# Sample loads and raw tokens issued earlier, key transposes later, and other PSUM banks for the first accumulators of the last part, in a two-layer decoder step

## The chip, the cores and the metric

The kernel runs on one core of one Trainium2 chip. The metric is the device time of one launch in microseconds, and the numbers of the kernel before are the median and the extremes of three runs, beside one execution that the hardware profiler recorded.

## What is computed

One inference step of a decoder with two layers, for 1024 prompt tokens and 8 samples that share all weights. Layer 0 has a gated linear recurrence (HGRN2, four heads of 128), layer 1 a stick-breaking attention over keys and values that layer 0 left; both have, beside it, a cross-attention of four heads into 256 memory rows, and a SwiGLU after it. The reference in short:

```python
def mem_attend(q, mk, mv):
    s = jnp.einsum('blhd,bmhd->bhlm', q, mk) * (q.shape[-1] ** -0.5)
    p = jax.nn.softmax(s, axis=-1)
    return jnp.einsum('bhlm,bmhd->blhd', p, mv)

def swiglu(h, w_gu, w_down):
    gate, up = jnp.split(h @ w_gu, 2, axis=-1)
    return (jax.nn.silu(gate) * up) @ w_down
...
    mk_p, mv_p = jnp.split(jnp.einsum('bmd,lde->lbme', mem_prompt, w_mem_kv), 2, axis=-1)
...
    for l in range(DEPTH):
        hn = rmsnorm(h, g[0])
        if l < N_A:
            mix, S = a_mixer(hn, w_in_a[l], ...)
        else:
            mix = b_mixer(hn, w_in_b[l - N_A], ...)
        h = h + rmsnorm(mix, g[1])
        h = h + rmsnorm(swiglu(rmsnorm(h, g[2]), w_gu[l], w_down[l]), g[3])
```

The prompt attends to memory keys and values projected from `mem_prompt`; each of the 8 samples has its own cached memory keys and values, and its own two pages of shared keys and values. All is float32.

## The kernel before

The tokens are two groups: group 0 is the first 512 prompt tokens, group 1 the last 512 and the 8 samples, 520 columns. Activations lie transposed, features on the partitions, in 8 tiles of 128 features. Every weight matrix is read in blocks of 512 rows by 128 columns (`w`), and each block is split into a high and a low half: `split_w` (L196) issues the DMA on SP, ACT casts (L206) and VectorE subtracts (L207). Activations are split likewise (L226 to L228). A product is then three matmuls, high by high, high by low and low by high, and a projection of 512 columns (`proj`, matmuls at L220) takes 24 matmuls for each of its output tiles and each half of the input features.

The order of the work is written out. Each stage is a generator that yields after each piece, and `weave` (L1617 to L1673) runs several generators side by side, each with a number of steps by which their pieces are spread over each other. The tile framework then makes one queue for each engine from it, and each engine works through its queue in order, waiting at semaphores. Three properties of the queues matter here:

- SP issues nearly all loads and stores, in order. A load whose tile is still in use holds all loads behind it.
- A tile comes from a pool of few buffers, taken in turn: T has 3 tiles, B 7, N 2, C 4, A 8; weights 5 raw and 5 split.
- PSUM has 8 banks: two pairs for projections (`mm`), three small ones (`s`, handed out by S()) and one for norms (`ns`). In the last part these pools are closed, and a pool called quads takes the same banks: q0 to q3, two of each.

The stages that the change touches:

- **Memory keys**, `mem_keys` (L815), once for each layer in the first core stage. A head's keys are 24 matmuls (L823) into one half of an `mm` pair. ACT copies them to a T tile (L828), and SP stores the tile (L829). PE then transposes the two halves of the copy into the other half of the same pair (L831), VectorE copies the result to another T tile (L833), and SP stores that to the output (L834).
- **First residual**, `residual` with `first` (L381). In layer 0 the residual stream is the raw input, which lies by tokens. Four loads of 128 tokens, 512 KB each (L388), are followed by a loop over the 8 feature tiles: four transposes into the norm bank (L396), an update by VectorE (L397) and an addition of the bank (L399). For group 1 the loads are at the start of the loop, after the key and value projections of group 0 and their stores.
- **Samples**, `sample_scores` (L935) and `sample_pv` (L960). A sample's scores are a product of its 256 cached keys with its query, broadcast to all partitions. For each of the 8 samples the loop loads the keys into a C tile (L1000 from the pages, L1014 from the memory cache), broadcasts the query by DMA into a B tile, multiplies (L954) and sums (L955) on VectorE; `sample_pv` does likewise with the values (L966, L967) and ends in matmuls (L969). These loops are woven with the feed-forward part of group 0 and, in layer 1, with the stick-breaking attention of the prompt. Of that, L1422 makes scores on PE, VectorE sums them along (L1440) and multiplies (L1443), PE transposes the result (L1449) and multiplies by the values (L1461).
- **Start of the last part.** `token_rows` and the final norms use L272, which sums squares with a matrix of ones, L283, which accumulates these squares on VectorE, and L416, which takes a projection out of its bank into the residual rows. `gate_up_q` (L468) makes the gate and the up half of a feed-forward block: `Q(0)`, `Q(1)` hold the gate's accumulators, `Q(2)`, `Q(3)` the up half's, and the matmuls are at L479.

The prediction also names the rows `w_in_a` and `w_gu`, the weights of the first projections and of the feed-forward part.

Of the kernel before, what the change touches and what calls it, by code (L numbers as in the profile page):

```python
# [9 lines left out]
F32 = mybir.dt.float32  # L10
# [8 lines left out]
P = 128  # L19
# [5 lines left out]
def tile_decoder(  # L25
# [6 lines left out]
    nc = tc.nc  # L32
# [348 lines left out]
    def residual(g, R, rstd, gc, store, acc=None, first=False):  # L381
        n = NG[g]
        w = D // 2 if first else n
        ht = [xpool.tile([P, 2, w], F32, tag=f"x{g}", name=nm("ht")) for _ in range(ND // 2)]
        for j in range(ND // 2):
            if first:
                t0 = g * G + j * P
                nc.sync.dma_start(ht[j].rearrange("p a n -> p (a n)"), x_prompt[0, t0 : t0 + P, :])  # L388
            else:
                nc.sync.dma_start(ht[j], hs[g][:, 2 * j : 2 * j + 2, :n])  # L390
        for k in range(ND):
            if first:
                ps = NS()
                for tb in range(CH):
                    xf = ht[tb].rearrange("p a n -> p (a n)")
                    nc.tensor.transpose(ps[:, tb * P : (tb + 1) * P], xf[:, k * P : (k + 1) * P], ident)  # L396
            nc.vector.scalar_tensor_tensor(R[k][:, :n], R[k][:, :n], gc(k), rstd[:, :n], op0=ALU.mult, op1=ALU.mult)  # L397
            if first:
                nc.vector.tensor_add(R[k][:, :G], R[k][:, :G], ps)  # L399
                if g:  # L400
                    nc.vector.tensor_add(R[k][:, G:n], R[k][:, G:n], xsraw[:, k, :])
            else:
                nc.vector.tensor_add(R[k][:, :n], R[k][:, :n], ht[k // 2][:, k % 2, :])
            if store:
                nc.sync.dma_start(hs[g][:, k, :n], R[k][:, :n])
            if acc is not None:
                sq_acc(acc, R[k][:, :n], k, n)
            yield
# [11 lines left out]
    class out_proj:  # L420


        def __init__(self, g, l, store, last=False):
            self.g, self.l, self.store, self.x, self.last = g, l, store, [], last
# [11 lines left out]
        def finish(self):  # L436
# [3 lines left out]
            yield from residual(g, self.R, rstd, lambda k: gcol(l, 1, k), not self.last, acc, l == 0)  # L440
# [27 lines left out]
    def gate_up_q(l, f, xt):  # L468

        h, n = PW[1], NG[1]  # L470
        sg = T()
        for j in range(2):
            w = split_w(w_gu[l], 0, ND, j * DFF + f * P)
            pp = [Q(2 * j + a) for a in range(2)]
# [340 lines left out]
    def mem_keys(l):  # L815
        for h in range(H):
            w = split_w(w_mem_kv[l], 0, ND, h * P)
            pb = mmp.tile([P, 2, 512], F32, tag="mm", name=nm("mm"))
            ps, pt = pb[:, 0, :], pb[:, 1, :]
# [10 lines left out]
            for tb in range(2):  # L830
                nc.tensor.transpose(pt[:, tb * P : (tb + 1) * P], src[:, tb * P : (tb + 1) * P], ident)  # L831
            tok = T()
            nc.vector.tensor_copy(tok[:, :NM], pt[:, :NM])  # L833
            nc.sync.dma_start(  # L834
                mk_prompt[l, 0, :, h, :].rearrange("(t p) d -> p t d", p=P),
                tok[:, :NM].rearrange("p (t d) -> p t d", t=2),
            )
            yield

# [95 lines left out]
    def sample_scores(q, load, sc):  # L935
# [13 lines left out]
        scv = sc.rearrange("p (k h b) -> p k h b", k=2, h=H)  # L949
        for b in range(NB):  # L950
            kt = load(b)
            qb = B()
            nc.sync.dma_start(qb, qd[b].partition_broadcast(P))
# [6 lines left out]
    def sample_pv(pT, load, xo, k0):  # L960
        po = NS()
        pv4 = pT.rearrange("p (k h b) -> p k h b", k=2, h=H)
        for b in range(NB):
            vt = load(b)
# [641 lines left out]
    for blk in range(2):  # L1606
# [28 lines left out]
    weave((chain(a1.merge(), a1.mem()), 12), (a1.mem_sample(), 20), (chain(f0.part(2), f0.part(3)), 16))  # L1635
    drain(f0.part(4))
    xk0, xb0 = [], []
    o1 = out_proj(1, 0, M)
# [24 lines left out]
        (chain(b1.sb(), b1.mem()), 40), (chain(b1.sb_sample(), b1.mem_sample()), 39),  # L1663
# [42 lines left out]
```

## Time and profile before

| | us |
|---|---|
| median of three runs | 2442.65 |
| lowest, highest | 2439.48, 2443.6 |
| the profiled execution | 2441.46 |
| its span, first to last instruction | 2439.7 |
| TensorE busy in it | 2410.5 |
| VectorE busy | 1561.0 |
| ScalarE busy | 1205.8 |

The mean granted clock of TensorE in the profiled execution is 0.998 of full speed. In the rows of the profile PE is TensorE's matmul, PEld its weight load, DVE VectorE, ACT ScalarE, POOL GpSimd and SP the queue that issues DMAs. A row of the timeline gives start, busy time, engine, line, operation, output and inputs, shapes and count, and in square brackets the idle time before it and what ended it. Times inside the text count from the start of the span.

### The profile page before, as it was taken

The page shows a single profiled execution, that of the slowest core. Times are in us where ns is not written, and L with a number is a line of the kernel's source. Part 1 is how long each engine was busy: PE and PEld are TensorE (multiplying, and loading weights), DVE is VectorE, ACT ScalarE, POOL GpSimd, SP SyncE. Part 2 cuts the span into 40 slices and gives each one's busy share as a digit, 9 for nine tenths or more (in the row PEclk, how much of TensorE's full clock was granted, in tenths as well). Part 3 has the DMA queues.
Part 4 walks back from the last instruction along what each step waited for, and adds up shares of the span by engine and source line. Part 5 has one row for each costly group of instructions (what it writes and reads, how often), then busy time and mean ns, then how long its engine had stood idle before and what let it go on. Part 6 is the DMA issues. An engine that isn't in the chain of part 4 may idle for free.

```text
span 2439.7 us, 40660 instructions
## 1 busy us (share of the span) xinstructions
PE 2410.5 (99%) x15483; PEld 2140.8 (88%) x15483; DVE 1561.0 (64%) x2688; ACT 1205.8 (49%) x2371; POOL 106.3 (4%) x167
## 2 busy tenths in 40 slices
PE   8999999999999999999999999999999999999998
PEld 6888988888877887999999989877787898999998
DVE  5777556765775676555544585677678548755665
ACT  5547544444444454555433454555454445554445
POOL 3000000000000000011111100021000000000000
PEclk9999999999999999999999999999999999999999
DMA  6353252254643446685778966544454234474542
GB/s 189 97 157 107 74 156 84 71 172 121 181 135 95 139 147 209 175 222 149 181 198 211 247 183 193 162 146 136 127 156 130 81 121 125 125 195 144 151 140 75
DMA packets 496726, 360.33 MB, mean 148 GB/s; under 512 B 19181, under 2 KB 443738, under 8 KB 496530
## 3 DMA queue, kind: packets, MB, share of 16 engines
q1 hardware_dynamic: 477864, 303.15, 41.7%
q0 software_dynamic: 18560, 54.53, 9.3%
q8 instruction: 122, 2.00, 0.3%
q14 instruction: 74, 0.61, 0.1%
q10 hardware_dynamic: 106, 0.04, 0.0%
HBM read 327.83 MB, written 75.96 MB: 166 GB/s over the span
## 4 chain that ended last, share of the span: by engine, by line
PE 92%; DVE 3%; DMA 2%; ACT 1%; issue 1%; SPq 0%; DVEq 0%; ACTq 0%; POOLq 0%; POOL 0%
PE mm L220 63%; PE q L521 7%; PE q L638 4%; PE q L479 2%; PE mm L1064 2%; PE s L914 1%; PE s L873 1%; PE s L1422 1%; PE s L1247 1%; PE mm L850 1%; PE q L722 1%; PE s L1461 1%; PE mm L823 1%; PE s L900 1%; DMA b<-qd 1%
## 5 line engine op out<-in xcount | busy, mean ns | idle before, releaser
L220 PE MATMUL mm<-x,ws 128*128 128x260 f32 (+1 forms) x7776 | 1330.5, 330 | 0.0
L220 PEld LDWEIGHTS mm<-x,ws 128*128 128x128 f32 x7776 | 1149.4, 188 | 143.1 <-issue 8.0
L206 ACT CAST ws<-w 128x512 fp32r<-128x512 f32 x704 | 414.8, 590 | 674.0 <-PE mm L220 556.4
L207 DVE TENSOR_TENSOR ws<-w,ws 128x512 fp32r<-128x512 f32 x704 | 456.6, 652 | 259.9 <-ACT ws L206 254.8
L220 PE MATMUL mm<-m,ws 128*128 128x512 f32 (+1 forms) x2112 | 391.9, 342 | 0.3 <-DVE r L416 0.3
L220 PEld LDWEIGHTS mm<-m,ws 128*128 128x128 f32 x2112 | 323.3, 188 | 47.0 <-issue 3.3
L512 DVE TENSOR_TENSOR ws<-w,ws 128x512 fp32r<-128x512 f32 x126 | 86.5, 691 | 59.7 <-ACT ws L511 57.0
L521 PE MATMUL q<-y,ws 128*128 128x260 f32 x864 | 112.9, 283 | 0.0
L511 ACT CAST ws<-w 128x512 fp32r<-128x512 f32 x126 | 78.0, 621 | 68.2 <-PE q L638 27.3
L521 PEld LDWEIGHTS q<-y,ws 128*128 128x128 f32 x864 | 107.6, 188 | 0.0
L638 PE MATMUL q<-m,ws 128*128 128x260 f32 x864 | 104.7, 282 | 0.0
L638 PEld LDWEIGHTS q<-m,ws 128*128 128x128 f32 x864 | 103.8, 188 | 0.3 <-ACT hT L454 0.2
L416 DVE TENSOR_TENSOR r<-r,mm 128x512 f32<-128x512 f32 (+1 forms) x96 | 66.0, 688 | 56.6 <-PE mm L220 55.5
L260 DVE TENSOR_SCALAR t<-mm 128x512 f32<-128x512 f32 (+1 forms) x74 | 51.2, 691 | 63.7 <-PE mm L220 63.7
L770 DVE TENSOR_TENSOR t<-t,mm 128x512 f32<-128x512 f32 (+1 forms) x66 | 45.5, 690 | 67.8 <-PE mm L220 67.2
L264 DVE TENSOR_TENSOR t<-t,t 128x512 f32<-128x512 f32 (+1 forms) x66 | 45.8, 693 | 65.7 <-ACT t L263 65.7
L521 PE MATMUL q<-x,ws 128*128 128x260 f32 x648 | 86.3, 282 | 0.0
L521 PEld LDWEIGHTS q<-x,ws 128*128 128x128 f32 x648 | 81.3, 188 | 0.0
L227 ACT CAST m<-t 128x512 fp32r<-128x512 f32 (+1 forms) x88 | 54.9, 624 | 24.7 <-DVE t L770 16.7
L1000 POOL DMA_INDIRECT c<-in_cache_sb_k,pidx x16 | 16.7, 1042 | 1120.8 <-DMA vsc<-c 910.9
L283 DVE TENSOR_TENSOR st<-st,n 128x512 f32<-128x512 f32 (+1 forms) x91 | 62.2, 691 | 3.1 <-ACT n L282 1.5
L228 DVE TENSOR_TENSOR m<-t,m 128x512 fp32r<-128x512 f32 (+1 forms) x88 | 60.9, 692 | 2.8 <-ACT m L227 1.6
(356 smaller groups left out, 2579.9 us busy)
## 6 DMA issues: line engine op xcount, KB each, us to landing
w<-in_w_gu SPq DMA_DIRECT2D x334, 256.0 KB, 3.3
w<-in_w_down SPq DMA_DIRECT2D x160, 256.0 KB, 2.9
w<-in_w_in_a SPq DMA_DIRECT2D x80, 256.0 KB, 2.9
wsum<-in_w_gu POOLq DMA_DIRECT2D x18, 1024.0 KB, 9.3
w<-wsum SPq DMA_DIRECT2D x72, 256.0 KB, 3.8
w<-in_w_o SPq DMA_DIRECT2D x64, 256.0 KB, 2.8
wsum<-in_w_gu POOLq DMA_DIRECT2D x12, 1280.0 KB, 10.9
w<-in_w_mem_kv SPq DMA_DIRECT2D x32, 256.0 KB, 3.2
```

The source lines that it names most:

```text
L206: nc.scalar.copy(ws[:, 0, :n, :], raw[:, :n, :])
L207: nc.vector.tensor_sub(ws[:, 1, :n, :], raw[:, :n, :], ws[:, 0, :n, :].bitcast(F32))
L220: nc.tensor.matmul(ps[:, a, : PW[g]], wt, xt[k][:, xi, o : o + PW[g]], start=(k == 0 and wi == 0), stop=(k == nk - 1 and wi == 2),)
L227: nc.scalar.copy(dst[0], src)
L228: nc.vector.tensor_sub(dst[1], src, dst[0].bitcast(F32))
L260: nc.vector.tensor_scalar(sv(x, g), pv(ps, g), -44.0, None, op0=ALU.max)
L283: nc.vector.tensor_add(acc[:, :n], acc[:, :n], t[:, :n])
L416: nc.vector.tensor_add(dst, dst, pv(ps, g))
L511: nc.scalar.copy(w[:, 0, :], src)
L512: nc.vector.tensor_sub(w[:, 1, :], src, w[:, 0, :].bitcast(F32))
L521: nc.tensor.matmul(ps[:, :h], w[:, wj, k * P : (k + 1) * P], x[:, xi, :], start=(first and k == 0 and wi == 0), stop=(k == 3 and wi == 2), ...
L638: nc.tensor.matmul(pp[a][:, :h], wt, mids[k][:, xi, a * h : (a + 1) * h], start=(k == 0 and wi == 0), stop=(k == nf - 1 and wi == 2),)
```

## The change

Four edits, which do not depend on each other:

1. `mem_keys`: the transposes, the copy and the output store of a head are issued after the next head's matmuls, and the transposes go to a small bank.
2. `raw_tokens`: the four loads of group 1's raw tokens are issued ahead of the last feed-forward pieces of group 0, into A tiles, and not in `residual`.
3. `gate_up_q`: the up half's accumulators are taken first and are `Q(0)`, `Q(1)`; the gate's are `Q(2)`, `Q(3)`.
4. The samples' loops issue the loads of sample b+1 (for the scores, also its query broadcast, now into an N tile) before the work on sample b. Each loop has one piece more, and the step counts in the weaves rise from 20 to 22 and from 39 to 43.

```diff
@@ -378,16 +378,19 @@
             out.append(x)
             yield
 
-    def residual(g, R, rstd, gc, store, acc=None, first=False):
+    def raw_tokens(g, tile):
+        ht = []
+        for j in range(CH):
+            ht.append(tile())
+            t0 = g * G + j * P
+            nc.sync.dma_start(ht[j].rearrange("p a n -> p (a n)"), x_prompt[0, t0 : t0 + P, :])
+        return ht
+
+    def residual(g, R, rstd, gc, store, acc=None, first=None):
         n = NG[g]
-        w = D // 2 if first else n
-        ht = [xpool.tile([P, 2, w], F32, tag=f"x{g}", name=nm("ht")) for _ in range(ND // 2)]
-        for j in range(ND // 2):
-            if first:
-                t0 = g * G + j * P
-                nc.sync.dma_start(ht[j].rearrange("p a n -> p (a n)"), x_prompt[0, t0 : t0 + P, :])
-            else:
-                nc.sync.dma_start(ht[j], hs[g][:, 2 * j : 2 * j + 2, :n])
+        ht = first or [xpool.tile([P, 2, n], F32, tag=f"x{g}", name=nm("ht")) for _ in range(ND // 2)]
+        for j in range(0 if first else ND // 2):
+            nc.sync.dma_start(ht[j], hs[g][:, 2 * j : 2 * j + 2, :n])
         for k in range(ND):
             if first:
                 ps = NS()
@@ -421,7 +424,7 @@
 
 
         def __init__(self, g, l, store, last=False):
-            self.g, self.l, self.store, self.x, self.last = g, l, store, [], last
+            self.g, self.l, self.store, self.x, self.last, self.ht = g, l, store, [], last, None
 
         def mm(self, xo, m0=0, m1=ND):
             g = self.g
@@ -437,7 +440,9 @@
             g, l = self.g, self.l
             rstd = rstd_from(self.acc, NG[g], 1.0 / D)
             acc = small([P, WID], tag="st", bufs=3)
-            yield from residual(g, self.R, rstd, lambda k: gcol(l, 1, k), not self.last, acc, l == 0)
+            if l == 0 and self.ht is None:
+                self.ht = raw_tokens(g, lambda: xpool.tile([P, 2, D // 2], F32, tag=f"x{g}", name=nm("ht")))
+            yield from residual(g, self.R, rstd, lambda k: gcol(l, 1, k), not self.last, acc, self.ht)
             r2 = rstd_from(acc, NG[g], 1.0 / D)
             yield
             yield from normed(g, self.R, r2, lambda k: gcol(l, 2, k), self.x, self.last)
@@ -469,9 +474,10 @@
 
         h, n = PW[1], NG[1]
         sg = T()
+        up = [Q(a) for a in range(2)]
         for j in range(2):
             w = split_w(w_gu[l], 0, ND, j * DFF + f * P)
-            pp = [Q(2 * j + a) for a in range(2)]
+            pp = up if j else [Q(2 + a) for a in range(2)]
             for k in range(ND):
                 wh, wl = w[k]
                 for wi, (wt, xi) in enumerate(((wh, 0), (wh, 1), (wl, 0))):
@@ -813,10 +819,23 @@
             yield
 
     def mem_keys(l):
+        late = []
+
+        def turned(h, src):
+            pt = S()
+            for tb in range(2):
+                nc.tensor.transpose(pt[:, tb * P : (tb + 1) * P], src[:, tb * P : (tb + 1) * P], ident)
+            tok = T()
+            nc.vector.tensor_copy(tok[:, :NM], pt[:, :NM])
+            nc.sync.dma_start(
+                mk_prompt[l, 0, :, h, :].rearrange("(t p) d -> p t d", p=P),
+                tok[:, :NM].rearrange("p (t d) -> p t d", t=2),
+            )
+
         for h in range(H):
             w = split_w(w_mem_kv[l], 0, ND, h * P)
             pb = mmp.tile([P, 2, 512], F32, tag="mm", name=nm("mm"))
-            ps, pt = pb[:, 0, :], pb[:, 1, :]
+            ps = pb[:, 0, :]
             for k in range(ND):
                 wh, wl = w[k]
                 for wi, (wt, xi) in enumerate(((wh, 0), (wh, 1), (wl, 0))):
@@ -827,15 +846,11 @@
             src = T()
             nc.scalar.copy(src[:, :NM], ps[:, :NM])
             nc.sync.dma_start(mks[l][:, h, :], src[:, :NM])
-            for tb in range(2):
-                nc.tensor.transpose(pt[:, tb * P : (tb + 1) * P], src[:, tb * P : (tb + 1) * P], ident)
-            tok = T()
-            nc.vector.tensor_copy(tok[:, :NM], pt[:, :NM])
-            nc.sync.dma_start(
-                mk_prompt[l, 0, :, h, :].rearrange("(t p) d -> p t d", p=P),
-                tok[:, :NM].rearrange("p (t d) -> p t d", t=2),
-            )
-            yield
+            if late:
+                turned(*late.pop())
+            late.append((h, src))
+            yield
+        turned(*late.pop())
 
     def mem_values(l):
         pb = mmp.tile([P, 2, 512], F32, tag="mm", name=nm("mm"))
@@ -947,10 +962,17 @@
         nc.sync.dma_start(qd, qt[:NB, :])
         yield
         scv = sc.rearrange("p (k h b) -> p k h b", k=2, h=H)
+        def both(b):
+            kt, qb = load(b), N()[:, :512]
+            nc.sync.dma_start(qb, qd[b].partition_broadcast(P))
+            return kt, qb
+
+        ahead = both(0)
+        yield
         for b in range(NB):
-            kt = load(b)
-            qb = B()
-            nc.sync.dma_start(qb, qd[b].partition_broadcast(P))
+            kt, qb = ahead
+            if b + 1 < NB:
+                ahead = both(b + 1)
             nc.vector.tensor_mul(kt, kt, qb.unsqueeze(1).to_broadcast([P, 2, 512]))
             nc.vector.tensor_reduce(
                 scv[:, :, :, b], kt.rearrange("p k (h d) -> p k h d", h=H), axis=AX.X, op=ALU.add
@@ -960,8 +982,12 @@
     def sample_pv(pT, load, xo, k0):
         po = NS()
         pv4 = pT.rearrange("p (k h b) -> p k h b", k=2, h=H)
+        ahead = load(0)
+        yield
         for b in range(NB):
-            vt = load(b)
+            vt = ahead
+            if b + 1 < NB:
+                ahead = load(b + 1)
             v4 = vt.rearrange("p k (h d) -> p k h d", h=H)
             nc.vector.tensor_mul(v4, v4, pv4[:, :, :, b].unsqueeze(3).to_broadcast([P, 2, H, P]))
             nc.vector.tensor_add(vt[:, 0, :], vt[:, 0, :], vt[:, 1, :])
@@ -1632,10 +1658,11 @@
     weave((a1.core(), 22), (f0.part(0), 9))
     a1.open()
     weave((a1.sample(), 6), (a1.gate(), 4), (f0.part(1), 9))
-    weave((chain(a1.merge(), a1.mem()), 12), (a1.mem_sample(), 20), (chain(f0.part(2), f0.part(3)), 16))
+    weave((chain(a1.merge(), a1.mem()), 12), (a1.mem_sample(), 22), (chain(f0.part(2), f0.part(3)), 16))
+    o1 = out_proj(1, 0, M)
+    o1.ht = raw_tokens(1, lambda: apool.tile([P, 2, D // 2], F32, tag="a", name=nm("ht")))
     drain(f0.part(4))
     xk0, xb0 = [], []
-    o1 = out_proj(1, 0, M)
     drain(o1.mm(a1.xo, 0, 1))
     weave((f0.finish(True), 9), (o1.mm(a1.xo, 1, 5), 4))
     weave((normed(0, f0.R, f0.r, gkvcol, xk0, True), 8), (o1.mm(a1.xo, 5, 7), 2))
@@ -1660,7 +1687,7 @@
     b1.open()
     f0 = ffn(0, 1, o0.x)
     weave(
-        (chain(b1.sb(), b1.mem()), 40), (chain(b1.sb_sample(), b1.mem_sample()), 39),
+        (chain(b1.sb(), b1.mem()), 40), (chain(b1.sb_sample(), b1.mem_sample()), 43),
         (chain(f0.part(0), f0.part(1), f0.part(2), f0.part(3)), 34),
     )
     o1 = out_proj(1, 1, A, True)
```

PE's queue where the last head of layer 0's keys stands (`memt` and `ws` are memory and weights, `t` the copy to be turned; the L1247 rows belong to the recurrence beside it). Before:

```order
L823 MATMUL mm_1004<-memt_841,ws_1001 128x256 x5
L1247 MATMUL s_1037<-a_664,b_986 128x128 x3
L831 MATMUL mm_1004<-ident,t_1029 128x128 x2
L1247 MATMUL s_1037<-a_664,b_986 128x128
L823 MATMUL mm_1059<-memt_838,ws_1051 128x256 x6
L823 MATMUL mm_1059<-memt_839,ws_1051 128x256 x6
L823 MATMUL mm_1059<-memt_840,ws_1056 128x256 x6
L823 MATMUL mm_1059<-memt_841,ws_1056 128x256 x6
L1247 MATMUL s_1092<-a_747,b_987 128x128 x3
L831 MATMUL mm_1059<-ident,t_1084 128x128 x2
L1247 MATMUL s_1092<-a_747,b_987 128x128
L220 MATMUL mm_1114<-x_261,ws_1106 128x512 x3
```

The same place of PE's queue after:

```order
L842 MATMUL mm_999<-memt_841,ws_996 128x256 x6
L827 MATMUL s_1027<-ident,t_978 128x128 x2
L1273 MATMUL s_1033<-a_664,b_981 128x128 x4
L842 MATMUL mm_1055<-memt_838,ws_1047 128x256 x6
L842 MATMUL mm_1055<-memt_839,ws_1047 128x256 x6
L842 MATMUL mm_1055<-memt_840,ws_1052 128x256 x6
L842 MATMUL mm_1055<-memt_841,ws_1052 128x256 x6
L827 MATMUL s_1083<-ident,t_1024 128x128 x2
L1273 MATMUL s_1089<-a_747,b_982 128x128 x4
L220 MATMUL mm_1111<-x_261,ws_1103 128x512 x3
```

Behind the 24 matmuls of `mm_1059` stood the transposes of that same head (`t_1084`); now those of the head before (`t_1024`, the copy of `mm_999`) stand there, in a bank of their own.

PE's queue at the start of the last part (`q` are the accumulators of the gate and, at L272, of the sums; `st` the accumulated squares). Before:

```order
L220 MATMUL mm_20218<-m_20015,ws_20215 128x512 x3
L479 MATMUL q_20276<-x_20075,ws_20268 128x260
L479 MATMUL q_20277<-x_20075,ws_20268 128x260
...
L479 MATMUL q_20276<-x_20129,ws_20268 128x260
L272 MATMUL q_20251<-st_20030,ones 128x512
L479 MATMUL q_20277<-x_20129,ws_20268 128x260
```

And after:

```order
L220 MATMUL mm_20226<-m_20023,ws_20223 128x512 x3
L485 MATMUL q_20286<-x_20083,ws_20278 128x260 x3
L485 MATMUL q_20286<-x_20088,ws_20278 128x260 x3
L485 MATMUL q_20286<-x_20137,ws_20278 128x260 x3
L485 MATMUL q_20286<-x_20142,ws_20278 128x260 x3
L485 MATMUL q_20286<-x_20191,ws_20283 128x260 x3
L272 MATMUL q_20259<-st_20038,ones 128x512
L485 MATMUL q_20287<-x_20083,ws_20278 128x260 x3
```

The two gate accumulators no longer alternate: 15 matmuls go to the first, then comes L272, and the second begins behind it. In both orders 15 gate matmuls stand ahead of L272.

VectorE's queue in layer 1's sample stage (`c` are a sample's keys, `b` or `n` its query, `sc` the scores; an L260 row begins a feed-forward step). Before, one step:

```order
L954 TENSOR_TENSOR c_15886<-c_15886,b_15889 128x1024
L260 TENSOR_SCALAR t_15928<-mm_15903 128x512
L955 TENSOR_REDUCE sc_15778<-c_15886 128x8
...
L954 TENSOR_TENSOR c_15994<-c_15994,b_15997 128x1024
L955 TENSOR_REDUCE sc_15778<-c_15994 128x8
L260 TENSOR_SCALAR t_16036<-mm_16011 128x512
```

After, the same scores:

```order
L260 TENSOR_SCALAR t_15934<-mm_15909 128x512
...
L976 TENSOR_TENSOR c_16088<-c_16088,n_16091 128x1024
L976 TENSOR_TENSOR c_16195<-c_16195,n_16198 128x1024
...
L977 TENSOR_REDUCE sc_15786<-c_16088 128x8
...
L977 TENSOR_REDUCE sc_15786<-c_16195 128x8
...
L976 TENSOR_TENSOR c_16222<-c_16222,n_16225 128x1024
L260 TENSOR_SCALAR t_16042<-mm_16017 128x512
```

Before, about one sample stands between two L260 rows; after, two, three and three samples stand in three consecutive steps. On SP the loads of raw tokens, which stood behind the stores of the value projection (L1379), now stand between loads of `w_in_a`, `w_down` and `w_gu`, two of them before and two behind the loads of the next feed-forward pieces' first `w_gu` blocks.

## The prediction

> **What bounds the kernel now.** I read the page's head and chain first, to learn which engine's waits are worth anything.
>
> ```profile
> span 2439.7 us, 40660 instructions
> PE 2410.5 (99%) x15483; PEld 2140.8 (88%) x15483; DVE 1561.0 (64%) x2688; ACT 1205.8 (49%) x2371; POOL 106.3 (4%) x167
> PE 92%; DVE 3%; DMA 2%; ACT 1%; issue 1%; SPq 0%; DVEq 0%; ACTq 0%; POOLq 0%; POOL 0%
> ```
>
> TensorE is busy for 99% of the span and carries 92% of the chain that ends last. No part of the change takes a matmul away, so it can only shorten the places where PE stands still. Next, PE's waits over the whole span (total, count, longest, in us):
>
> ```profile
> PE s L1449 <- DVE b L1443: 4.1, 8, 1.5
> PE ns L396 <- DMA ht<-in_x_prompt: 2.5, 2, 1.7
> PE mm L831 <- ACT t L828: 2.1, 1, 2.1
> PE q L479 <- DVE r L416: 1.7, 1, 1.7
> ```
>
> Ahead of these stands only a 7.6 us wait at the start, outside the change. The four lines answer to the four edits, and together they hold 10.4 us. The profiled execution took 2441.46 us (1.76 around its span), 1.19 under the median of the runs, 2442.65. A measurement of this kernel tells about 0.2%, 4.9 us, from no change.
>
> **Edit 1: memory key transposes.** PE, ACT and SP around the wait:
>
> ```profile
> 103.14 0.42 SPq L834 DMA_DIRECT2D out_mk_prompt<-t  x1
> 103.14 5.93 DMA out_mk_prompt<-t
> 109.16 0.37 ACT L828 COPY t<-mm 128x256 f32<-128x256 f32 x1 [3.15 <-DMA out_mk_prompt<-t]
> 109.59 0.44 PE L831 MATMUL mm<-ident,t 128*128 128x128 f32 x2 [2.12 <-ACT t L828]
> 110.01 7.36 PE L220 MATMUL mm<-x,ws 128*128 128x512 f32 x24
> ```
>
> A head's transposes need ACT's copy, the copy needs one of three T tiles, and that tile waits for an earlier head's store, issued at 103.14 and 5.93 us under way. After, the transposes behind the last head's 24 products are those of the head before, copied long ago. Their own bank, a small one, has three turns. ACT's copy may still wait for a store, but PE has the 24 products of the next projection (7.36 us here) meanwhile. Gain 2.1. Its two transposes and the copy are moved, not multiplied: cost 0.
>
> The wait has a tail, which the clock column (PEclk, behind the counts) shows:
>
> ```profile
> core 0: us, PE busy (x) PEld busy (x) DVE busy (x) ACT busy (x) POOL busy (x), PEclk, DMA share, GB/s
> 106.00:113.00 7.00, 4.88 (x26) 4.09 (x25) 5.30 (x12) 1.35 (x4) 0.00 (x0) 0.85 0.61 181
> 113.00:120.00 7.00, 7.00 (x41) 6.16 (x40) 3.51 (x8) 2.26 (x5) 0.00 (x0) 0.91 0.26 76
> 936.00:944.00 8.00, 5.52 (x25) 3.53 (x24) 3.38 (x6) 2.59 (x5) 2.15 (x2) 1.00 1.06 366
> 2062.00:2070.00 8.00, 7.43 (x57) 6.98 (x58) 8.00 (x14) 5.40 (x11) 0.00 (x0) 1.00 0.24 68
> ```
>
> Behind the 2.12 us wait the granted clock falls: 0.15 x 7 + 0.09 x 7 = 1.7 us of full-speed work lost. Behind the 1.7 us waits of the last two rows it stays at 1.00. I count these 1.7 as part of the gain. [...]
>
> **Edit 2: raw tokens earlier.**
>
> ```profile
> 931.00 1.86 SPq L388 DMA_DIRECT2D ht<-in_x_prompt  x4
> 940.67 0.33 PE L396 MATMUL ns<-ident,ht 128*128 128x128 f32 x1 [1.74 <-DMA ht<-in_x_prompt]
> 943.13 0.33 PE L396 MATMUL ns<-ident,ht 128*128 128x128 f32 x1 [0.74 <-DMA ht<-in_x_prompt]
> 940.57 0.75 DVE L397 SCALAR_TENSOR_TENSOR m<-m,par,st 128x520 f32<-128x520 f32 x1
> 943.49 0.69 DVE L399 TENSOR_TENSOR m<-m,ns 128x512 f32<-128x512 f32 x1 [2.18 <-PE ns L396]
> 383.80 11.09 PE mm L220 x48
> ```
>
> The four 512 KB loads go out when the transposes are nearly due, into a DMA share of 1.06. After, they are issued some 330 us ahead, between weight loads, and they land long before. Both stops at the transposes go: 2.5. What is late next is DVE, which frees the one normalising bank. Without the stop its L399 of the first tile would end near 941.2. PE meanwhile has about ten projection products between two groups, 10 x 0.231 (11.09/48) = 2.3 us from 938.93 (940.67 less the wait), to 941.2. So it just fits, later groups by as little; I take 2.4, with 1.7 (the first stop alone) and 2.9 as ends. The cost at their new place: all of PE's waits from 550 to 770 are
>
> ```profile
> PE s L1024 <- DVE b L1021: 0.6, 1, 0.6
> PE mm L220 <- DVE r L416: 0.3, 1, 0.3
> ```
>
> none of them for a weight. SP issues four more loads of about 0.47 us (1.86/4), and 2 MB pass beside weight loads that PE doesn't wait for: 0. What covers them is the lead of the weight tiles; if it were gone and one load came late by a whole stop, the price would be that of the first stop above, 1.7.
>
> **Edit 3: banks of the last part.**
>
> ```profile
> 2057.64 3.18 PE L220 MATMUL mm<-m,ws 128*128 128x512 f32 x13
> 2061.74 0.68 DVE L416 TENSOR_TENSOR r<-r,mm 128x512 f32<-128x512 f32 x1
> 2062.57 2.03 PE L479 MATMUL q<-x,ws 128*128 128x260 f32 x15 [1.75 <-DVE r L416]
> 2063.55 0.68 DVE L283 TENSOR_TENSOR st<-st,n 128x512 f32<-128x512 f32 x1
> 2064.43 1.02 PE L272 MATMUL q<-st,ones 128*128 128x512 f32 x2
> ```
>
> The gate products wait for L416 to empty their bank. With other banks they may start when the projection ends, at 2060.8. But the order puts 15 of them ahead of L272, which sums `st` and needs the last L283, ending at 2064.23 whatever PE does. Fifteen products are at most 2.03 us and by PE's rows about 1.8: they end at 2062.7, and PE, in order, stands before L272 until 2064.4. The stop moves; it does not go. Gain 0, with -0.2 and +1.75 (L272 not in the way) as ends.
>
> **Edit 4: samples' loads ahead.**
>
> ```profile
> L954 DVE TENSOR_TENSOR c<-c,b 128x1024 f32<-128x1024 f32 x16 | 19.5, 1221 | 7.5 <-DMA b<-qd 7.5
> L955 DVE TENSOR_REDUCE sc<-c 128x8 f32<-128x1024 f32 x16 | 19.4, 1214 | 0.2
> 1832.42 1.23 DVE L954 TENSOR_TENSOR c<-c,b 128x1024 f32<-128x1024 f32 x1 [1.23 <-DMA b<-qd]
> 1835.87 0.68 DVE L1443 TENSOR_TENSOR b<-b,b 128x512 f32<-128x512 f32 x1
> 1836.70 0.63 PE L1449 MATMUL s<-ident,b 128*128 128x128 f32 x4 [1.48 <-DVE b L1443]
> ```
>
> In the stretch from 1540 to 1950 DVE stands 7.5 us for the query broadcast, in its queue ahead of L1443, on which PE waits. At 1832 the 1.23 us idle becomes most of PE's 1.48. After, the broadcast is a step old, and that stop falls to the few tenths that every fourth step has anyway (the eight waits sum to 4.1; about 0.4 each beside the longest). I count 1.4 here and 0.5 for the sample stage of layer 0, where the same idle stands ahead of a 0.6 us wait: 1.9. Ends: 4.7 (4.1 + 0.6, all of it) and below nothing, as the order now puts two or three samples' L954 and L955 into consecutive feed-forward steps (the rival below).
>
> Sum: 2.1 + 1.7 + 2.4 + 0 + 1.9 = 8.1. Against the profiled execution 2433.4, against the median 2442.65 - 8.1 = **2434.5**, which I forecast.
>
> **The rivals.** (a) The samples do not pay: DVE's idle goes but its work fills the hole, since 2.43 us of L954 and L955 sit where the wait was. Then 2434.5 + 1.9 = 2436.4, and with a wait of 2 more 2438.4. For it: two to three samples in a row.
>
> (b) The key copies hold ACT longer. ACT runs its queue in order, so a copy that waits 3.15 us for a store also holds the weight casts behind it, and PE runs dry at L220 in place of L831, clock included: 2442.65 - 2.4 - 1.9 = 2438.4. For it: T tiles are still three and each store still takes one.
>
> (c) The stop before L272, now about 1.7 to 1.9 us, crosses the length at which the clock falls (between 1.75 and 2.12 here): +1.7, 2436.2. (d) L272 is not late: -1.7, 2432.8.
>
> (e) Slower: the sample stage overfills VectorE.
>
> ```profile
> 1554.00:1567.00 13.00, 13.00 (x58) 10.22 (x57) 7.15 (x13) 6.48 (x13) 0.00 (x0) 1.00 0.46 141
> 1567.00:1579.00 12.00, 12.00 (x57) 9.92 (x56) 9.76 (x15) 7.03 (x13) 2.49 (x2) 1.00 0.37 115
> 1571.12 0.69 DVE L1443 TENSOR_TENSOR b<-b,b 128x512 f32<-128x512 f32 x1
> 1577.81 0.60 PE L1449 MATMUL s<-ident,b 128*128 128x128 f32 x4
> ```
>
> A step of 12 to 13 us holds 7.15 us of DVE work without a sample and 9.76 with one. After, eight samples stand in three consecutive steps: 3 x 7.15 + 8 x 2.43 = 40.9 us against 3 x 12.5 = 37.5 of PE. DVE falls 3.4 us behind, and this L1443 has a margin of 6 (1571.81 to 1577.81), so PE should not notice. It decides where the lag passes the margin of the next L1443: 6 here, but none at the tiles on which PE waits already. Were the margin none throughout, both rounds of scores would hand PE their lag, 2 x 3.4 = 6.8, in waits near 2 us, with a clock fall of 1.7 behind each of four, 6.8 again. Edit 4 then gains nothing: 2434.5 + 1.9 + 13.6 = 2450.
>
> (f) The change does not do what it says, the early loads landing late for instance: 2.4 of the sum goes, 2436.9.
>
> **How the numbers follow.** The forecast with all four terms as sized, 2432 to 2437, gets 0.42; (a) 0.18, (b) 0.14, (c) 0.07, (d) 0.06, (f) 0.04, (e) 0.09. "Faster by over 0.2%" means under 2437.8: the forecast, (c), (d), (f) and most of (a) and a little of (b), 0.72. Within 0.2%: the rest of (a) and (b), 0.19. Slower: (e), 0.09. The range runs from 2430.5 (the forecast with the upper ends of edits 2 and 4) to 2441 (case (b) with the loss of (a)), leaving out (e) and the extremes.
>
> **What would show it.** In the profile after: no wait at the key transposes and a clock of 1.00 from 106 to 120; no wait on the raw tokens' loads, and the waits of the normalising bank's transposes below 0.3; a new wait of PE at L272's line for DVE, near 1.7 us, at the last part's start, and none at its first gate products; DVE's idle on the query broadcast near zero from 1540 to 1950 and L1449's longest wait under 0.8. Waits of over 2 us at L1449's line, or a clock below 1 in the sample stage, would prove me wrong towards (e); a wait at L220 for casts near 110, towards (b).

## The result and the profile after

The changed kernel took 2433.15 us in the median of 8 runs (2431.55 to 2434.6), the kernel before 2441.03 in the median of its 8 (2437.53 to 2443.6): 7.9 us less. The ratio is 0.9965, with a 95% interval of 0.9956 to 0.9974. Lines of the changed kernel carry numbers up to 27 higher than before.

TensorE's longest waits in the profile after (total, count, longest, in us):

```profile
PE s L145 <- DVE rr L335: 7.8, 1, 7.8
PE s L1475 <- DVE b L1469: 3.0, 9, 0.5
PE q L485 <- DVE r L419: 1.8, 1, 1.8
PE ns L365 <- DVE xtok L340: 1.1, 3, 0.5
PE ns L995 <- DVE c L993: 0.8, 1, 0.8
```

Of the four lines that answered to the four edits, two are gone: the key transposes and the raw tokens. One lost its longest member: L1449, now L1475, has 0.5 in place of 1.5. One is what it was: the gate's first products, L479, now L485. New is a wait of 0.8 at the samples' values of layer 0 (L995).

The key transposes after, on PE and ACT, then the windows with the clock (PEclk is the number behind the counts):

```profile
104.25 3.09 PE L842 MATMUL mm<-memt,ws 128*128 128x256 f32 x24
107.17 0.38 PE L827 MATMUL s<-ident,t 128*128 128x128 f32 x2
107.39 1.07 PE L1273 MATMUL s<-a,b 128*128 128x128 f32 x8
108.22 5.80 PE L220 MATMUL mm<-x,ws 128*128 128x512 f32 x24
```

```profile
107.42 0.37 ACT L847 COPY t<-mm 128x256 f32<-128x256 f32 x1 [0.85 <-PE mm L842]
```

```profile
106.00:113.00 7.00, 7.00 (x43) 6.13 (x42) 7.00 (x15) 2.51 (x5) 0.00 (x0) 1.00 0.78 238
113.00:120.00 7.00, 7.00 (x54) 6.65 (x53) 5.42 (x12) 3.34 (x7) 0.00 (x0) 1.00 0.20 43
```

PE runs through, ACT's copy waits for its products and no longer for a store, and the clock stays full. The 24 projection products take 5.80 us where they took 7.36.

The raw tokens after, SP's four loads and PE's first groups:

```profile
571.20 0.50 SPq L386 DMA_DIRECT2D ht<-in_x_prompt  x1
574.79 0.50 SPq L386 DMA_DIRECT2D ht<-in_x_prompt  x1
...
604.71 0.34 SPq L386 DMA_DIRECT2D ht<-in_x_prompt  x1
...
607.74 0.34 SPq L386 DMA_DIRECT2D ht<-in_x_prompt  x1
```

```profile
935.07 0.61 PE L399 MATMUL ns<-ident,ht 128*128 128x128 f32 x4
935.44 2.58 PE L220 MATMUL mm<-x,ws 128*128 128x512 f32 x10
937.86 0.60 PE L399 MATMUL ns<-ident,ht 128*128 128x128 f32 x4
938.21 1.19 PE L220 MATMUL mm<-x,ws 128*128 128x512 f32 x4
```

No group waits, neither for a load nor for the bank.

The start of the last part after, PE and then DVE:

```profile
2054.58 2.05 PE L485 MATMUL q<-x,ws 128*128 128x260 f32 x15 [1.75 <-DVE r L419]
2056.47 1.02 PE L272 MATMUL q<-st,ones 128*128 128x512 f32 x2
```

```profile
2053.75 0.68 DVE L419 TENSOR_TENSOR r<-r,mm 128x512 f32<-128x512 f32 x1
```

The wait neither went nor moved. It is 1.75 us long as before, at the same place, ended by the same instruction, the last that takes a projection out of its bank, though the accumulators of these products now have other banks than before.

The samples of layer 1, VectorE's groups (idle before them and its main releaser at the end of the row):

```profile
L976 DVE TENSOR_TENSOR c<-c,n 128x1024 f32<-128x1024 f32 x16 | 19.3, 1220 | 1.9 <-DMA n<-qd 1.9
```

VectorE stands 1.9 us for the broadcast queries where it stood 7.5.

It is one wait, for the query of the first sample of a loop:

```profile
1556.85 1.22 DVE L976 TENSOR_TENSOR c<-c,n 128x1024 f32<-128x1024 f32 x1 [1.92 <-DMA n<-qd]
```

So each edit left the mark that its step named, but for the banks, and the idle for the broadcast fell less than the "near zero" of the forecast. Whether each is worth what the step said, one profile of each kernel can't say. That is what the experiments are for.

### The profile page after: what moved, and what is told of

Same layout as the page of the kernel before. It is cut to its first block, busy times and chain, and to the rows that moved or that the text cites. A ratio compares the mean times of both kernels' runs of the same rounds, so it can differ in the third digit from the quotient of the medians.

```text
span 2431.6 us, 40665 instructions
## 1 busy us (share of the span) xinstructions
PE 2408.9 (99%) x15483; PEld 2140.8 (88%) x15483; DVE 1559.9 (64%) x2688; ACT 1207.1 (50%) x2371; POOL 110.0 (5%) x167
## 4 chain that ended last, share of the span: by engine, by line
PE 91%; issue 4%; DVE 2%; DMA 1%; ACT 1%; POOL 0%; SPq 0%; DVEq 0%; POOLq 0%; ACTq 0%
PE mm L220 63%; PE q L527 7%; PE q L644 4%; PE q L485 2%; PE mm L1090 2%; PE s L929 1%; PE s L888 1%; PE s L1273 1%; PE mm L842 1%; PE mm L865 1%; PE q L728 1%; PE s L1448 1%; PE s L1487 1%; PE s L915 1%; PE s L1475 1%
## 5 line engine op out<-in xcount | busy, mean ns | idle before, releaser
L260 DVE TENSOR_SCALAR t<-mm 128x512 f32<-128x512 f32 (+1 forms) x74 | 51.2, 692 | 63.9 <-PE mm L220 63.9
```

The costliest lines, as they stand in the source:

```text
L260: nc.vector.tensor_scalar(sv(x, g), pv(ps, g), -44.0, None, op0=ALU.max)
```

## The experiments

Twelve runs: each edit alone on the kernel before, each edit undone in the changed kernel, the changed kernel again, and two further kernels, one of them twice. The kernel before ran beside each four; its median was 2440.74 for the first four, 2439.84 for the next and 2439.92 for the last. A 95% interval of one kernel's ratio is about 0.1% to each side, 2.2 us, so a single comparison does not resolve a gain of one or two microseconds; the argument rests on pairs of them and on the profiles. The diffs show the core of each edit.

### Memory keys alone

Only this edit:

```diff
...
+            if late:
+                turned(*late.pop())
+            late.append((h, src))
...
+        turned(*late.pop())
```

> Only the memory keys' edit on the kernel before. If the wait of 2.1 us before the transposes and the clock fall behind it are both its doing, the time is 3.8 to 4.1 us under the kernel before, near 2437, the clock from 106 to 120 us is 1.00, and TensorE waits at no line of mem_keys for ScalarE's copy. If the clock fall has another cause, only 2.1 go and the clock still drops near 111. If a store that holds a T tile now holds ScalarE and with it the weight casts, TensorE waits at L220 there instead and nothing is gained.

Measured: 2439.34, 1.4 under before; ratio 0.9993 (0.9984 to 1.0002). In the profile the wait at the keys is gone and the clock is 1.00 from 106 to 120. But this kernel keeps the old samples, and there its profile differs from that of before:

```profile
1835.78 0.63 PE L1458 MATMUL s<-ident,b 128*128 128x128 f32 x4 [2.29 <-DVE b L1452]
```

```profile
1828.00:1836.00 8.00, 5.71 (x28) 4.30 (x28) 5.95 (x8) 2.56 (x5) 0.00 (x0) 1.00 0.40 125
1836.00:1844.00 8.00, 8.00 (x36) 6.54 (x35) 6.15 (x11) 3.75 (x8) 0.00 (x0) 0.79 0.49 164
```

The samples' wait is 2.29 us, not 1.48, and a clock fall follows it: 0.21 x 8 = 1.7 us. Neither has to do with the keys. The profile of before held the shortest sample wait of the five with the old loops.

### Raw tokens alone

```diff
...
+    o1 = out_proj(1, 0, M)
+    o1.ht = raw_tokens(1, lambda: apool.tile([P, 2, D // 2], F32, tag="a", name=nm("ht")))
     drain(f0.part(4))
```

> Only the early raw tokens. If the two stops of 1.74 and 0.74 us were the whole matter and the loads cost nothing at their new place, 2.4 to 2.9 us under before, near 2438.4, and no wait of TensorE from 575 to 620 us that was not there. If the 2 MB delay weights there, a new wait of up to 1.7 us at L220 takes it back: near 2440.

Measured: 2440.33, 0.4 under before; ratio 0.9999 (0.999 to 1.0008), so gains up to 2.4 are not excluded. No wait for the tokens and no new one for a weight: the stretch from the sums ahead of the residual to those behind it takes 23.95 us, not 26.79 as in the profile before. The old keys and the old samples here show waits of

```profile
110.51 0.44 PE L836 MATMUL mm<-ident,t 128*128 128x128 f32 x2 [1.51 <-ACT t L833]
...
1834.33 1.08 PE L1454 MATMUL s<-ident,b 128*128 128x128 f32 x4 [2.51 <-DVE b L1448]
```

The first is shorter than before's 2.12 and no fall follows it; the second is longer, and the clock is 0.79 from 1834 to 1842.

### The other banks alone

```diff
+        up = [Q(a) for a in range(2)]
...
-            pp = [Q(2 * j + a) for a in range(2)]
+            pp = up if j else [Q(2 + a) for a in range(2)]
```

> Only the other banks for the gate's accumulators. If the new pool as a whole waits for the last reader of the closed pools, the wait of 1.75 us stays at the first gate product (L481 here), ended by the same L416, and the time is that of before, 2441. If the wait moved to L272, as forecast, the same time with the stop at another row. If banks were the whole matter: 1.75 less, 2439.3.

Measured: 2440.63, 0.1 under before by the medians; ratio 1.0002 (0.9993 to 1.0011), no difference. The wait stays at the first gate product with 1.7. This profile holds a surprise on the keys, whose code is that of before:

```profile
107.38 0.84 PE L1248 MATMUL s<-a,b 128*128 128x128 f32 x6
108.13 0.44 PE L832 MATMUL mm<-ident,t 128*128 128x128 f32 x2
```

```profile
107.70 0.37 ACT L829 COPY t<-mm 128x256 f32<-128x256 f32 x1 [0.93 <-DMA out_mk_prompt<-t]
```

ACT waited 0.93 us for the store, not 3.15, and PE not at all. So the wait that the first step removed is there in some executions and not in others.

### Samples alone

```diff
+        ahead = both(0)
+        yield
         for b in range(NB):
...
+            kt, qb = ahead
+            if b + 1 < NB:
+                ahead = both(b + 1)
...
```

> Only the samples' loads a step ahead. By the forecast 1.9 us under before, near 2439.1, most of it the wait of 1.48 us at 1836, and VectorE's idle for the query broadcast near zero. If VectorE's crowded steps take it back, the waits at L1449's line (here shifted) sum to 4 us as before or more, and the time is 2441 or above. With the other three the four gains should add up to the 7.9 us of the whole change; if two of them share a gain the sum is larger.

Measured: 2436.12, 4.6 under before; ratio 0.998 (0.9971 to 0.9989). This is by far the largest part, and 2.4 times the forecast's term. The longest wait at the old L1449 is 0.5. The old keys show a wait of 1.9 here, with the clock at 1.00 behind it.

The four alone give 1.4 + 0.4 + 0.1 + 4.6 = 6.5, the whole 7.9; four intervals of 2.2 us cover the difference.

### Each edit undone

Raw tokens back in the residual:

```diff
...
+            if first:
+                t0 = g * G + j * P
+                nc.sync.dma_start(ht[j].rearrange("p a n -> p (a n)"), x_prompt[0, t0 : t0 + P, :])
...
-    o1.ht = raw_tokens(1, lambda: apool.tile([P, 2, D // 2], F32, tag="a", name=nm("ht")))
```

> The changed kernel with the raw tokens' loads back in the residual. If the early loads are worth what their stops cost (0.8 to 2.5 us in four profiles with the old loads), 1.9 above the changed kernel, near 2435.1 against 2433.15. If they are worth the 0.4 that they gave alone, because the loads at their new place cost something or another wait takes the gain, 2433.5.

Measured: 2434.43; ratio to before 0.9977 (0.9968 to 0.9986). That is 1.3 above the changed kernel's 2433.15. (This kernel and the next two ran beside a kernel before with 2439.84, not 2441.03. The changed kernel's later run, beside one with 2439.92, gave 2432.94, further down; against it each of the three differences is 0.2 larger.) The wait for the tokens is 0.4 in its profile.

Old memory keys:

```diff
-            if late:
-                turned(*late.pop())
-            late.append((h, src))
+            for tb in range(2):
+                nc.tensor.transpose(pt[:, tb * P : (tb + 1) * P], src[:, tb * P : (tb + 1) * P], ident)
...
```

> The changed kernel with the old memory keys. Theory now: the wait before the transposes differs from launch to launch (0 to 2.1 us in four profiles) and the clock fall follows only some of them, so on the median 1.4 to 2 above the changed kernel, near 2434.8. By the forecast, wait and fall in every launch, 3.8 above: 2437.0.

Measured: 2434.51; ratio to before 0.9977 (0.9968 to 0.9986): 1.4 above the changed kernel. The wait is 0.8 in its profile, with no fall.

Old sample loops:

```diff
-        def both(b):
-            kt, qb = load(b), N()[:, :512]
+        for b in range(NB):
+            kt = load(b)
+            qb = B()
             nc.sync.dma_start(qb, qd[b].partition_broadcast(P))
-            return kt, qb
...
-            kt, qb = ahead
-            if b + 1 < NB:
-                ahead = both(b + 1)
...
```

> The changed kernel with the old sample loops. Theory now: the wait near 1831 us is usually 2.1 to 2.5 us, with a clock fall of 1.7 behind most of those, not the 1.5 of the profile before, so 4.5 above the changed kernel, near 2437.7. By the forecast's size, 1.9 above: 2435.1.

Measured: 2437.97; ratio to before 0.9991 (0.9982 to 1.0): 4.8 above the changed kernel. The sample wait is 2.10 in its profile with no fall behind it. But a fall stands behind another wait, that of the last part's first products:

```profile
2057.93 2.48 PE L485 MATMUL q<-x,ws 128*128 128x260 f32 x15 [1.75 <-DVE r L419]
```

```profile
2054.00:2062.00 8.00, 6.25 (x28) 4.50 (x27) 8.00 (x14) 3.72 (x7) 0.00 (x0) 0.83 0.24 68
2062.00:2070.00 8.00, 8.00 (x66) 8.00 (x65) 6.53 (x12) 5.43 (x9) 0.00 (x0) 0.95 0.21 60
```

It cost 0.17 x 8 + 0.05 x 8 = 1.8 us. The same 1.75 us wait had a clock of 1.00 behind it in the profile before.

Old banks:

```diff
-            pp = up if j else [Q(2 + a) for a in range(2)]
+            pp = [Q(2 * j + a) for a in range(2)]
```

> The changed kernel with the old accumulators' banks. If the wait at the first gate product belongs to the pool and not to the bank, the same time as the changed kernel, within 0.5, and the same wait of 1.75 us at the same row. If the other banks are worth something that the profiles did not show, 1 or more above it.

Measured: 2432.61; ratio to before 0.997 (0.9959 to 0.9981), and the same wait of 1.7 at the same row. Beside it on the same chip stood the changed kernel again:

> The changed kernel once more, unchanged, on the chip that runs the next three, so that they have it beside them: near 2433.2, no clock fall in most launches, and the wait of 1.75 us at the first gate product.

Measured: 2432.94; ratio 0.9973 (0.9963 to 0.9982). That is 7.0 under the kernel before beside it, so the whole change was measured at 7.9 and at 7.0. The banks are worth nothing that either comparison shows.

### Why the gate's wait stayed: two pools

In the changed kernel all eight banks of the last part belong to one pool, opened after all old pools are closed. This kernel closes the small banks' pools first and opens a pool over them, then closes the pairs and opens a second one; the gate takes its accumulators from the first.

```diff
...
-        return single[0].tile([P, 512], F32, tag=f"q{i}", name=nm("q"))
+        return single[i in (0, 3)].tile([P, 512], F32, tag=f"q{i}", name=nm("q"))
...
-        up = [Q(a) for a in range(2)]
+        up = [Q(0), Q(3)]
...
-            pp = up if j else [Q(2 + a) for a in range(2)]
+            pp = up if j else [Q(1), Q(2)]
...
-    single.append(ctx.enter_context(tc.tile_pool(name="quads", bufs=2, space=PSUM)))
+    single.append(ctx.enter_context(tc.tile_pool(name="quads", bufs=2, space=PSUM, side="right")))
+    pairs.close()
+    single.append(ctx.enter_context(tc.tile_pool(name="quadp", bufs=2, space=PSUM)))
```

> The changed kernel with the last part's banks opened as two pools, one over the small banks and one over the pairs, and the gate's accumulators in the first. If the wait of 1.75 us at the first gate product was the whole new pool waiting for the last reader of the old ones, it goes, and some 34 gate products run ahead of the sums at L273, which are then late no more. What is next is VectorE, which makes the normalised tiles: a wait of about 0.9 us for the tile after the fourth pair. So 0.5 to 1.2 less than the changed kernel, near 2432.3. If the pools are not the cause the wait stays and the time is 2433.15.

Its profile, the same place on PE, and a later one:

```profile
2045.76 5.27 PE L221 MATMUL mm<-m,ws 128*128 128x512 f32 x22
2050.87 4.23 PE L486 MATMUL q<-x,ws 128*128 128x260 f32 x34
2054.94 1.02 PE L273 MATMUL q<-st,ones 128*128 128x512 f32 x2
2055.40 6.79 PE L486 MATMUL q<-x,ws 128*128 128x260 f32 x52
...
2087.50 1.09 PE L1564 MATMUL q<-ident,r 128*128 128x128 f32 x8 [0.21 <-DVE t L495]
2088.98 1.15 PE L1564 MATMUL q<-ident,r 128*128 128x128 f32 x8 [0.39 <-ACT c L1567]
2090.31 0.51 PE L528 MATMUL q<-x,ws 128*128 128x260 f32 x2 [0.19 <-ACT c L1567]
```

The wait is gone: the gate starts as the projection ends, 34 products run ahead of the sums, and the sums don't wait. Other banks in the same pool left it where it was, at 1.75 us in two kernels; two pools removed it. So the wait belonged to the pool, not to the bank. The wait for VectorE's tiles that I expected behind it is not there. Instead new waits of 0.21, 0.39 and 0.19 stand 30 us later, where group 0's results are turned for the output. In the changed kernel the same 16 transposes stand later in PE's queue, behind 88 more gate products, and wait for nothing:

```profile
2101.46 1.91 PE L1563 MATMUL q<-ident,r 128*128 128x128 f32 x16
2103.13 1.70 PE L527 MATMUL q<-x,ws 128*128 128x260 f32 x12
```

There they take 1.67 us. With two pools 3.25 us pass from the first transpose to the next gate products, of which the two products between take an estimated 0.3 (12 take 1.70 above): about 1.3 more, and the 0.21 ahead of them.

Measured: 2431.75; ratio 0.9968 (0.9957 to 0.998), against 0.9965 for the changed kernel. To compare both on one chip it ran again:

> The two pools beside the changed kernel on one chip. If the gate's wait of 1.75 us was real time and nothing behind it takes it back, 1.2 to 1.8 under the changed kernel, near 2431.7. If VectorE, which is full in that stretch, or the later token rows take it back, within 0.5 of it.

Measured: 2432.19; ratio 0.997 (0.9958 to 0.9982), 0.75 under the changed kernel beside it. That lies inside both intervals. From the sums at 2028 us to the last product of the kernel, two executions with two pools take 394.81 and 394.77 us, two of the changed kernel 395.07 and 395.04. So the wait of 1.75 us is gone at its place, but nearly all of it is given back later: 0.25 to 0.3 is left.

### Which of the samples' loops

The changed kernel with the values' loop loading in its own step again:

```diff
-        ahead = load(0)
-        yield
         for b in range(NB):
-            vt = ahead
-            if b + 1 < NB:
-                ahead = load(b + 1)
+            vt = load(b)
...
```

> The changed kernel with the look-ahead in the scores' loop alone; the values' loop loads in its own step again, and the step counts are 21 and 41. If the query broadcast is what VectorE stood for (7.5 us of idle in the profile before against 4.3 and 3.5 for the values), the samples' gain stays nearly whole: within 0.7 of the changed kernel. If the values' loads carry part of it, up to 2 above, with new waits at the values' line (L995 in the changed kernel).

Measured: 2432.7; ratio 0.997 (0.9957 to 0.9982), 0.2 under the changed kernel beside it. VectorE's idle in layer 1's scores:

```profile
L976 DVE TENSOR_TENSOR c<-c,n 128x1024 f32<-128x1024 f32 x16 | 19.2, 1216 | 2.0 <-DMA n<-qd 2.0
```

So the gain stays without the values' look-ahead, within the 2 us that such a comparison can tell, and in the traces too: layer 1's sample stretch, measured below, takes 530.6 us here and 530.3 to 530.6 with both. It is the scores' look-ahead that pays. Whether the query broadcast or the keys' load of that loop does it was not taken apart; the profile names the broadcast.

## Why the prediction was right, and where it was wrong

The time forecast, 2434.5, was 1.35 above the measured one, and the gain of 8.1 stands beside a measured 7.9 (7.0 in the second comparison). Its terms were not right one by one.

PE does nearly the same work in the same order in all kernels, so one can measure stretches of its queue, from one row of the sums at L272 to another. These are the rows that bound the stretches in the kernel before, then in the changed one; the last stretch ends at the first gate product, 2062.57 and 2054.58:

```profile
330.86 1.12 PE L272 MATMUL ns<-st,ones 128*128 128x512 f32 x2
360.88 1.10 PE L272 MATMUL ns<-st,ones 128*128 128x512 f32 x2
841.45 1.02 PE L272 MATMUL ns<-st,ones 128*128 128x512 f32 x2
935.79 1.02 PE L272 MATMUL ns<-st,ones 128*128 128x512 f32 x2
962.58 1.10 PE L272 MATMUL ns<-st,ones 128*128 128x512 f32 x2
1530.37 1.13 PE L272 MATMUL ns<-st,ones 128*128 128x512 f32 x2 [0.29 <-DVE st L283]
```

```profile
327.75 1.12 PE L272 MATMUL ns<-st,ones 128*128 128x512 f32 x2
357.76 1.10 PE L272 MATMUL ns<-st,ones 128*128 128x512 f32 x2
837.97 1.02 PE L272 MATMUL ns<-st,ones 128*128 128x512 f32 x2
932.34 1.02 PE L272 MATMUL ns<-st,ones 128*128 128x512 f32 x2
956.27 1.10 PE L272 MATMUL ns<-st,ones 128*128 128x512 f32 x2
1524.22 1.12 PE L272 MATMUL ns<-st,ones 128*128 128x512 f32 x2 [0.30 <-DVE st L283]
```

The table has the lengths in us in all profiles of this case: of those kernels that have the old code in the stretch, and of those that have the new (the one with the look-ahead in the scores alone counted here; the two profiles with two pools have no such end of the last stretch). The first stretch holds the start of the kernel as well; its spread with the new code, 2.0, is not the keys'. The last two columns are the gain of the means and the forecast's term.

| stretch, and what lies in it | old code: range, mean | new code: range, mean | gain | forecast |
|---|---|---|---|---|
| start to 330.86, keys | 327.9 to 330.9, 329.6 (5) | 326.2 to 328.2, 327.6 (9) | 1.9 | 3.8 |
| 360.88 to 841.45, layer 0's samples | 480.3 to 480.8, 480.6 (5) | 479.3 to 480.2, 479.7 (9) | 0.9 | 0.5 |
| 935.79 to 962.58, raw tokens | 24.5 to 27.2, 25.9 (5) | 23.9 to 24.0, 23.9 (9) | 2.0 | 2.4 |
| 1530.37 to 2062.57, layer 1's samples | 532.2 to 535.1, 533.6 (5) | 530.3 to 530.6, 530.4 (7) | 3.2 | 1.4 |

The gains sum to 8.0. The stretches between these agree to 0.3 us in all kernels, and so does the last part of those with one pool, but for the clock fall told above. In the two profiles of before and after alone the four differences are 3.1, 0.4, 2.9 and 1.8, each within 0.7 of its term. So the terms, read from one profile, described that execution well; what they could not show is that another execution has other waits.

**Keys: mechanism right, size wrong.** The term was 2.1 + 1.7 = 3.8; alone the edit gave 1.4, undone it cost 1.4, and the stretch shrank by 1.9. Five profiles with the old keys show waits of 2.12, 1.51, none, 1.93 and 0.83, a mean of 1.3, and a clock fall behind one in five: 1.3 + 1.7/5 = 1.6. I had taken the one profile at hand, which happened to hold the longest wait and the only fall, for every launch. The sentence that failed is "I count these 1.7 as part of the gain": the trace showed one execution, not every launch. The rival that ACT's copies would hold the casts did not come: in the profile after the copy waits 0.85 us for its products and no longer for a store.

**Raw tokens: mechanism right, size about right.** The term was 2.4; alone the edit gave 0.4, undone it cost 1.3, neither resolved by its interval of 2.2. In the profiles with the old loads the waits sum to 2.5, 2.0, 1.9, 0.8 and 0.4, a mean of 1.5, and the stretch is 2.0 longer. The loads cost nothing seen at their new place, and no group waits, though ten projection products took 2.58 us and not the 2.3 reckoned. The three larger sums of waits belong to kernels with the old sample loops, the two smaller to kernels with the look-ahead. In all five the loads are issued 4.6 to 4.8 us before the sums (931.00 and 935.79 in the profile before), so what differs is when they land; whether the sample loops have to do with it stays open.

**Banks: the sum's zero came true for a wrong reason.** I wrote that the first products might start at once and the stop would move to L272. The stop did not move: with one pool the first gate product waited 1.75 us for the last reader of the closed pools, with the old banks and with the new, and with two pools it did not wait. Where the first products did start at once, L272 came behind 34 of them and was not late either: the order of 15 products that I read from the queue holds for one pool only.

**Samples: mechanism right, size too small.** The term was 1.9 for both layers; alone the edit gave 4.6, undone it cost 4.8, and the two stretches shrank by 0.9 + 3.2 = 4.1. The step said that the wait of 1.48 falls to a few tenths. So it did, but 1.48 was the shortest of five: the others are 2.29, 2.51, 2.12 and 2.10, with a fall of 1.7 behind two. Layer 0's samples lost waits of 0.6 and 0.3 and got one of 0.8 or less.

**The slower rival** did not come. Its price hung on VectorE's lag reaching PE at L1449's line. The longest wait there is 0.5, none of over 2 us stands in the sample stage, and the clock is 1.00: the margin held with two and three samples a step. The first rival, that VectorE's work fills the hole, did not come either, as the sample stretches show.

**The clock.** The forecast put the bound between 1.75 and 2.12 us. The runs refute a bound: waits of 2.10, 2.12 and 1.93 had no fall behind them, one of 1.75 had one, and of a dozen waits of 1.7 or 1.75 at the last part's start it was the only one. Its fall cost 1.8, and those behind waits of 2.12, 2.29 and 2.51 cost 1.7 each. Behind the start of the kernel no wait was longer than 2.51. What decides whether the clock falls behind a wait was not shown.

That the forecast came so close is in part luck: by the stretches it had the keys 1.9 and the tokens 0.4 too large, and the samples 2.2 too small. Its range, too, was a little wider than its own terms give: the forecast with the upper ends of edits 2 and 4 is 2431.2, not 2430.5, and case (b) with the loss of (a) is 2440.3, not 2441.

## What to carry to other kernels

A wait in one profile, where a transfer stood behind it, was here a draw, not a price. Take its size from several executions before summing; kernels that leave that place alone give them for nothing. Where no single comparison resolves a gain, compare the lengths of one stretch, between two fixed rows, over all profiles on record: kernels that differ elsewhere count too. The wait behind the query broadcast stood in all five profiles with the old loops, 1.48 to 2.51 us; the one behind the keys' store in four of five, none to 2.12, and they paid accordingly. And before giving a tile another bank or buffer to free it, see whether the wait is for the buffer or for the pool that it is in.

## What the runs showed of the hardware

The clock fell behind waits of 1.75, 2.12, 2.29 and 2.51 us and stayed at 1.00 behind others of 1.75 and 2.12, so length alone did not decide; each fall cost 1.7 to 1.8 us of full-speed work beside the wait itself. The store of the turned keys held ACT for 3.15 us in one execution and 0.93 in that of another kernel with the same code there, so that a wait of TensorE of 2.12 us was there or not.
